# Decay sums of both triangles side by side in two-part products, key blocks on ScalarE, two gate weights off GpSimd, constants loaded in the first stage

## The chip, the cores and the metric

The kernel runs on one core of a Trainium2 chip. The metric is device time in microseconds (us), the median of several executions of the whole kernel. A profiled execution gives the trace: each instruction's start and duration on TensorE (PE), VectorE (DVE), ScalarE (ACT), GpSimd (POOL) and SyncE (SP), which here only issues transfers.

## The reference

One layer of a decoder works on 512 prompt tokens and 8 x 4 sample tokens with one set of weights. Half of its heads are sparse attention (NSA), half gated linear attention (GLA); then come an output projection, a gated feed-forward part, and a per-layer embedding gate. What matters here is the GLA part, whose decays are sums of logarithms within chunks of 32 tokens, and the mixer's output:

```python
def step(S, blk):
    qc, kc, vc, ac = blk
    b = jnp.cumsum(ac, axis=1)
    qe = qc * jnp.exp(b)
    ke = kc * jnp.exp(-b)
    att = jnp.where(causal, jnp.einsum('bihd,bjhd->bhij', qe, ke), 0.0)
    o = jnp.einsum('bhij,bjhv->bihv', att, vc) + jnp.einsum('bihd,bhdv->bihv', qe, S)
    b_last = b[:, -1]
    kd = kc * jnp.exp(b_last[:, None] - b)
    S = S * jnp.exp(b_last)[..., None] + jnp.einsum('bjhd,bjhv->bhdv', kd, vc)
    return S, o
...
o_g = (rmsnorm(o_gla, gla_norm) * jax.nn.silu(g_gla)).reshape(B, T, GLA_V_DIM)
return jnp.concatenate([o_nsa, o_g], axis=-1) @ w_o
```

The last step of all is `rmsnorm(h, norm_final)`, whose result is the output yT.

## The kernel before

Activations stand with features on the partitions: 1024 features are 8 tiles of 128, and the 544 columns (512 prompt, 32 sample) are worked in two halves of 256 and 288. Projections are exact to float32 by two parts: a weight tile `wraw` of 128 x 1024 is split into `wh` and `wl`, activations into `xh` and `xl`, and three products (wh xh, wh xl, wl xh) of a reduced-precision float32 type are added in PSUM (`acc3`). The split of a weight is a cast on ScalarE and a subtraction on VectorE, or, with `lo=POOL`, both on GpSimd, the subtraction in four pieces (`load_w`). A product of plain float32 shows two records in the trace.

The work is staged: input statistics, NSA projections and key compression; scores and softmax of the prompt; GLA projections (`pj` tiles of qg, kg, vg); the GLA stage; the output projection (`pk`); the feed-forward part (`pg`, `pu`, `pd`); embedding gate and final norm. Each engine has one queue and works it in order. A scheduler sets the order of each queue from the program and from priorities; `tc.issue_after` and `together` tie some instructions to others.

In the GLA stage stand side by side:

- The four gate weights gg0 to gg3 (`tile_gg`): each is fetched one ahead (`raws`), split on GpSimd, and multiplied with all 544 columns; `ev_silu` makes the gate `om_g` of it.
- The sample values (`s_values`): score tiles are transposed (`sT`, `pT`) and multiplied with value pages `vch` into `sO`. For each row of four pages SyncE loads three and GpSimd gathers one (`load_page`, `gather_page`); there are four buffers. The result is copied to `Os` on ScalarE and transposed (`sOT`).
- The GLA itself. The log decays `ls` come back from DRAM. `sps` are the sums for the sample tokens, with the small triangle `tri4`. For each pair of heads (ip 0 and 1) `gla_front` makes the sums for the prompt with two triangles, `bps` and `rps`, their exponentials `E`, `En`, `X`, and the transposed keys (`kdp`, then X again); `gla_states` copies the keys of each of four blocks into a block-diagonal tile `kdz` (L1095: four copies of 32 rows, two on GpSimd, two on ScalarE), multiplies them with the values (`U`, PSUM) and chains the states S on VectorE; `gla_out` makes the outputs (`go`, `U`), their norms (`og`, `gst`: square, sum, power, scaling; the power is on GpSimd) and `gla_gate` transposes them (`ogp`) and multiplies them with the gate. The sample tokens' part (`oiq`, `oip`, `vb`, `kd`) uses `bmask`, `glah` and `tri4`.

After it, the mixer's output is split again into `xh2` and `xl2`, which take over the buffers of `xh` and `xl`, and the first products of `pk` run on the parts of the first 256 columns that are there (`early_k`). In the last stage `finish` scales h by the broadcast reciprocal norm `bc` and stores it.

Of the kernel before, what the change touches and what calls it, by code (L numbers as in the profile page):

```python
# [9 lines left out]
F32 = mybir.dt.float32  # L10
F32R = mybir.dt.float32r
I32 = mybir.dt.int32
AF = mybir.ActivationFunctionType
ALU = mybir.AluOpType
# [21 lines left out]
def kernel(ctx: ExitStack, tc: tile.TileContext, i: dict, o: dict):  # L36
# [591 lines left out]
    later[3][1]()  # L628
    compress_prompt()
# [372 lines left out]
    def tile_gg(j, lo=POOL):  # L1002
        w = load_w(None, 1024, lo, raw=raws[j])
        if j < 3:
            raws.append(fetch(i["win_fm"][FM.index(f"gg{j + 1}")], 1024))
        fm_tile(None, ev_silu(j), w, then=tick)
# [6 lines left out]
    tri4 = gp.tile([32, 3, 32], F32, name="tri4")  # L1013
    SP.dma_start(tri4, i["tri4"])
    bmask = gp.tile([128, 8], F32, name="bmask")
    SP.dma_start(bmask, i["bmask"])
    glan = gp.tile([128, 1], F32, name="glan")
    SP.dma_start(glan, i["glan"])
    glah = gp.tile([128, 1], F32, name="glah")
    DVE.tensor_scalar_mul(glah, glan, 0.5)  # L1020
# [39 lines left out]

    def gla_front(ip):
        cs = slice(ip * 128, ip * 128 + 128)
        bps, rps = g1("bps"), g1("rps")
        for t in range(4):
            mm(bps[:, t * 128:t * 128 + 128], ls[:, t, cs], tri[:, 0, :])
# [3 lines left out]
        ACT.activation(E, bps, AF.Exp, scale=-1.0)  # L1069
        ACT.activation(En, bps, AF.Exp)  # L1070
        for t in range(4):
            mm(rps[:, t * 128:t * 128 + 128], ls[:, t, cs], tri[:, 1, :])
        ACT.activation(X, rps, AF.Exp, scale=-1.0)
# [14 lines left out]
    def gla_states(ip, ec, kdt):  # L1088
        S = gp.tile([128, 17, 128], F32, name="S", bufs=2)
        POOL.memset(S[:, 0, :], 0.0)  # L1090
        for t in range(4):
            kz = kdz[t % 2]
            for c in range(4):
                cp_ = slice(32 * c, 32 * c + 32)
                (ACT.copy if c % 2 else POOL.tensor_copy)(kz[cp_, c, :], kdt[cp_, t, :])  # L1095
# [127 lines left out]

    def split_o(k, hf):
# [9 lines left out]
    def early_k(k0, k1):  # L1234
        for mt in range(2):
            for k in range(k0, k1):
                acc3(parts[mt], HALF[0][1], w_wo[mt], k, xh2, xl2, k, 0, k == 0, False)
# [3 lines left out]
    for k in range(4):  # L1241
        split_o(k, 0)
    w_wo = [load_w(i["wo"][mt], 1024) for mt in range(2)]
# [3 lines left out]
    early_k(0, 4)  # L1247
    for k in (4, 5):
        split_o(k, 0)
# [171 lines left out]
    def finish(dg, hf):  # L1421
# [4 lines left out]
        ACT.copy(r[:, :n], bc[:, :n])  # L1426
        ys = [pl_.tile([128, 2, 288], F32, name="y", bufs=5) for _ in range(5)]
        where = {0: (0, 0), 4: (2, 0), 1: (1, 0), 5: (2, 1), 2: (3, 0), 3: (3, 1), 6: (4, 0), 7: (4, 1)}
        for k, (z, j) in where.items():
# [183 lines left out]
```

## Time and profile before

| | |
|---|---|
| runs | 907.25, 898.73, 907.13 us (median 907.13) |
| profiled execution | 902.78 us, its span 901.0 us |
| TensorE busy | 857.9 us, 95% of the span |
| VectorE, ScalarE, GpSimd busy | 55%, 40%, 17% |
| mean granted clock of TensorE | 0.98 of full speed |

The span runs from the first to the last instruction of the core; the executions' time has 1.8 us around it. A busy share is a mean over all stages. The granted clock is given as a share of 2.4 GHz; 0.5 is the lower level of 1.2 GHz. In a row of the timeline the number in brackets is the engine's idle time ahead of it, with what ended it.

### The profile page before, as it was taken

How to read it: one execution, taken by the hardware profiler on the slowest of the kernel's cores; microseconds unless marked ns; L12 is line 12 of the kernel's file. 1: busy time of each engine (PE TensorE's matmuls, PEld its weight loads, DVE VectorE, ACT ScalarE, POOL GpSimd, SP SyncE). 2: the span in 40 equal slices, each digit the busy share in tenths (PEclk: the TensorE clock that was granted, in tenths of full speed). 3: DMA queues.
4: the chain of work that ended last, by engine and by line, in shares of the span. 5: the costliest groups of instructions: out<-in, count | busy, mean ns of one | idle time of the engine just before them, and what ended most of it. 6: DMA issues, size and time to landing. Idle time of an engine off the chain costs nothing.

```text
span 901.0 us, 18098 instructions
## 1 busy us (share of the span) xinstructions
PE 857.9 (95%) x6872; PEld 794.4 (88%) x6872; DVE 496.4 (55%) x1204; ACT 364.7 (40%) x898; POOL 151.6 (17%) x196
## 2 busy tenths in 40 slices
PE   5999999999999988899999999999999999999995
PEld 5899987777777756799999999999999999999994
DVE  6646367778665634584555555555554333335654
ACT  7344377678755501452332323333232222224322
POOL 3544153000026215250000000000000000002511
PEclk9999999999998969999999999999999999999998
DMA  8677423232205232561233333322223232234111
GB/s 253 190 228 214 126 79 113 80 101 60 92 2 169 84 122 71 169 235 60 83 111 101 117 118 117 109 96 101 75 90 85 88 105 77 86 103 142 48 54 47
DMA packets 58822, 99.09 MB, mean 110 GB/s; under 512 B 11319, under 2 KB 40264, under 8 KB 58352
## 3 DMA queue, kind: packets, MB, share of 16 engines
q1 hardware_dynamic: 55296, 90.33, 31.5%
q0 software_dynamic: 2192, 5.90, 2.3%
q10 hardware_dynamic: 1248, 1.70, 0.5%
q8 instruction: 54, 0.88, 0.4%
q14 instruction: 32, 0.26, 0.1%
HBM read 91.74 MB, written 10.37 MB: 113 GB/s over the span
## 4 chain that ended last, share of the span: by engine, by line
PE 79%; DVE 6%; issue 4%; POOL 4%; ACT 3%; DMA 2%; SPq 1%; DVEq 0%; POOLq 0%; ACTq 0%
PE pg L57 17%; PE pd L57 15%; PE pu L57 15%; PE pj L57 9%; PE pk L57 5%; PE cps L57 4%; PE sc L57 3%; PE pO L57 2%; PE pT L776 2%; PE U L57 2%; PE go L57 1%; POOL xc L98 1%; DVE xl L259 1%; PE sS L57 1%; PE sO L57 1%
## 5 line engine op out<-in xcount | busy, mean ns | idle before, releaser
L132 ACT CAST wh<-wraw 128x1024 fp32r<-128x1024 f32 (+1 forms) x89 | 91.6, 1030 | 166.9 <-issue 73.9
L137 DVE TENSOR_TENSOR wl<-wraw,wh 128x1024 fp32r<-128x1024 f32 (+1 forms) x85 | 101.8, 1198 | 87.7 <-ACT wh L132 86.8
L57 PE MATMUL pg<-xh,wh 128*128 128x256 f32 (+1 forms) x400 | 115.7, 289 | 0.0
L57 PE MATMUL pg<-xl,wh 128*128 128x256 f32 (+1 forms) x400 | 115.2, 288 | 0.0
L57 PE MATMUL pg<-xh,wl 128*128 128x256 f32 (+1 forms) x400 | 114.6, 286 | 0.0
L57 PE MATMUL pd<-hh,wl 128*128 128x256 f32 (+1 forms) x352 | 101.8, 289 | 0.0
L57 PE MATMUL pd<-hl,wh 128*128 128x256 f32 (+1 forms) x352 | 101.6, 289 | 0.0
L57 PE MATMUL pd<-hh,wh 128*128 128x256 f32 (+1 forms) x352 | 101.6, 289 | 0.0
L57 PE MATMUL pu<-xh,wh 128*128 128x256 f32 (+1 forms) x352 | 101.5, 288 | 0.0
L57 PE MATMUL pu<-xl,wh 128*128 128x256 f32 (+1 forms) x352 | 101.3, 288 | 0.0
L57 PE MATMUL pu<-xh,wl 128*128 128x256 f32 (+1 forms) x352 | 100.8, 286 | 0.0
L57 PE MATMUL pj<-xh,wh 128*128 128x256 f32 (+1 forms) x272 | 82.0, 304 | 10.0 <-ACT wh L132 8.1
L176 POOL TENSOR_TENSOR prs<-pst,mhalf 128x2 f32<-128x2 f32 (+1 forms) x9 | 6.0, 672 | 451.8 <-DVE pst L175 451.8
L57 PE MATMUL pj<-xl,wh 128*128 128x256 f32 (+1 forms) x272 | 80.5, 298 | 0.0
L57 PE MATMUL pj<-xh,wl 128*128 128x256 f32 (+1 forms) x256 | 76.9, 300 | 1.3 <-DVE wl L137 1.2
L57 PEld LDWEIGHTS pg<-xh,wl 128*128 128x128 f32 x400 | 75.3, 188 | 0.0
L57 PEld LDWEIGHTS pg<-xl,wh 128*128 128x128 f32 x400 | 75.1, 188 | 0.0
L57 PEld LDWEIGHTS pg<-xh,wh 128*128 128x128 f32 x400 | 75.0, 188 | 0.1
L57 PEld LDWEIGHTS pd<-hh,wh 128*128 128x128 f32 x352 | 66.3, 188 | 0.1
L57 PEld LDWEIGHTS pu<-xh,wl 128*128 128x128 f32 x352 | 66.3, 188 | 0.0
L57 PEld LDWEIGHTS pd<-hl,wh 128*128 128x128 f32 x352 | 66.3, 188 | 0.0
L57 PEld LDWEIGHTS pd<-hh,wl 128*128 128x128 f32 x352 | 66.2, 188 | 0.0
(400 smaller groups left out, 2065.9 us busy)
## 6 DMA issues: line engine op xcount, KB each, us to landing
wraw<-in_wg SPq DMA_DIRECT2D x22, 512.0 KB, 3.4
wraw<-in_wu SPq DMA_DIRECT2D x22, 512.0 KB, 3.3
wraw<-in_win_fm SPq DMA_DIRECT2D x17, 512.0 KB, 3.3
wraw<-in_wd SPq DMA_DIRECT2D x16, 512.0 KB, 3.5
xc<-in_pgc SPq DMA_DIRECT2D x32, 128.0 KB, 2.6
kch<-in_pgk SPq DMA_DIRECT2D x64, 64.0 KB, 2.0
wraw<-in_wo SPq DMA_DIRECT2D x8, 512.0 KB, 4.2
wraw<-in_wpg SPq DMA_DIRECT2D x8, 512.0 KB, 4.1
```

The costliest lines, as they stand in the source:

```text
L57: pe[0] = PE.matmul(out, lhsT, rhs, start=start, stop=stop)
L98: return POOL.indirect_dma_start(out=dst, out_offset=None, in_=src.rearrange("a p c -> (a p) c"), in_offset=bass.IndirectOffsetOnAxis(ap=p ...
L132: ACT.copy(wh[:, :n], raw[:, :n])
L137: lo_[0] = DVE.tensor_sub(wl[:, :n], raw[:, :n], wh[:, :n])
L176: POOL.tensor_tensor(r[0:m, b:e], a[0:m, b:e], mhalf[0:m, b:e], op=ALU.pow)
L259: DVE.scalar_tensor_tensor(xl[:, k, c0:c1], v, gk, xh[:, k, c0:c1], op0=ALU.mult, op1=ALU.subtract)
L776: PE.transpose(tp[:, 128 * r:128 * r + 128], Ps[r][b][:, 128 * kt:128 * kt + 128], ident)
```

## The change

1. `tri4`, `bmask` and `glan` are loaded in the first stage and not in the GLA stage; `glah` is made there too.
2. `ls` is split into two parts (`lsh` by a cast on ScalarE, `lsl` on VectorE in place), the two triangles are cast side by side into `trr`, and each block of 128 columns takes two products of 128 x 256 (`brs`) for both triangles. The six exponentials of a pair are of 128 x 256 (three of 128 x 512 before), X first.
3. All copies into `kdz` are on ScalarE.
4. gg2 and gg3 are split on ScalarE and VectorE; gg3's call fetches the first tile of wo.
5. The two parts of the first four tiles of the mixer's output, first half, go to buffers of `E` and `En` (`split_first`), from which the first products of `pk` read; GpSimd copies them to xh2 and xl2 later, for the other products.
6. In `finish` for the last half, VectorE scales six tiles from the PSUM tile `bc` itself; a second broadcast serves the copy for GpSimd's two (three before). Stores go to SyncE's and ScalarE's queues in turn.

```diff
@@ -626,6 +626,14 @@
     later[2][1]()
     fm_tile("q1", ev_q(1), then=lambda hf: block(5 + hf))
     later[3][1]()
+    tri4 = op_.tile([32, 3, 32], F32, name="tri4")
+    SP.dma_start(tri4, i["tri4"])
+    bmask = op_.tile([128, 8], F32, name="bmask")
+    SP.dma_start(bmask, i["bmask"])
+    glan = op_.tile([128, 1], F32, name="glan")
+    SP.dma_start(glan, i["glan"])
+    glah = op_.tile([128, 1], F32, name="glah")
+    DVE.tensor_scalar_mul(glah, glan, 0.5)
     compress_prompt()
     gates()
     wg3 = decay_factors()
@@ -999,10 +1007,9 @@
     raws = [fetch(i["win_fm"][FM.index("gg0")], 1024)]
-    def tile_gg(j, lo=POOL):
-        w = load_w(None, 1024, lo, raw=raws[j])
-        if j < 3:
-            raws.append(fetch(i["win_fm"][FM.index(f"gg{j + 1}")], 1024))
+    def tile_gg(j):
+        w = load_w(None, 1024, POOL if j < 2 else None, raw=raws[j])
+        raws.append(fetch(i["win_fm"][FM.index(f"gg{j + 1}")] if j < 3 else i["wo"][0], 1024))
         fm_tile(None, ev_silu(j), w, then=tick)
@@ -1010,14 +1017,6 @@
     SP.dma_start(ls, lsd)
     tri = gp.tile([128, 3, 128], F32, name="tri")
     SP.dma_start(tri, i["tri"])
-    tri4 = gp.tile([32, 3, 32], F32, name="tri4")
-    SP.dma_start(tri4, i["tri4"])
-    bmask = gp.tile([128, 8], F32, name="bmask")
-    SP.dma_start(bmask, i["bmask"])
-    glan = gp.tile([128, 1], F32, name="glan")
-    SP.dma_start(glan, i["glan"])
-    glah = gp.tile([128, 1], F32, name="glah")
-    DVE.tensor_scalar_mul(glah, glan, 0.5)
     qs = gp.tile([128, 2, NS], F32, name="qs")
@@ -1058,19 +1057,34 @@
     for z in range(2):
         POOL.memset(kdz[z], 0.0)
+    lst = gp.tile([128, 1280], F32R, name="lst", tag="S", bufs=2)
+    lsh, trr = lst[:, 0:1024].rearrange("p (t c) -> p t c", t=4), lst[:, 1024:1280]
+    lsl = ls[:, 0:4, :].bitcast(F32R)
+    ACT.copy(trr, tri[:, 0:2, :].rearrange("p a c -> p (a c)"))
+    ACT.copy(lsh, ls[:, 0:4, :])
+    DVE.tensor_sub(lsl, ls[:, 0:4, :], lsh)
     def gla_front(ip):
         cs = slice(ip * 128, ip * 128 + 128)
-        bps, rps = g1("bps"), g1("rps")
-        for t in range(4):
-            mm(bps[:, t * 128:t * 128 + 128], ls[:, t, cs], tri[:, 0, :])
+        both = []
+        for z in range(2):
+            ps = g1("brs")
+            for t in range(2):
+                for w in (lsh, lsl):
+                    mm(ps[:, 256 * t:256 * t + 256], w[:, 2 * z + t, cs], trr, start=w is lsh, stop=w is lsl)
+            both.append(ps.rearrange("p (t a c) -> p a t c", t=2, a=2))
+        def half(t, z):
+            return t[:, 256 * z:256 * z + 256].rearrange("p (t c) -> p t c", t=2)
         E = gp.tile([128, SEQ], F32, name="E", bufs=2)
         En = gp.tile([128, SEQ], F32, name="En", bufs=2)
         X = gp.tile([128, SEQ], F32, name="X", bufs=1)
-        ACT.activation(E, bps, AF.Exp, scale=-1.0)
-        ACT.activation(En, bps, AF.Exp)
-        for t in range(4):
-            mm(rps[:, t * 128:t * 128 + 128], ls[:, t, cs], tri[:, 1, :])
-        ACT.activation(X, rps, AF.Exp, scale=-1.0)
+        for z in range(2):
+            ACT.activation(half(X, z), both[z][:, 1], AF.Exp, scale=-1.0)
+            ACT.activation(half(E, z), both[z][:, 0], AF.Exp, scale=-1.0)
+            ACT.activation(half(En, z), both[z][:, 0], AF.Exp)
         DVE.tensor_mul(X, kg[:, ip, :SEQ], X)
         kdp = g1("kdp")
         for t in range(4):
@@ -1092,7 +1106,7 @@
             kz = kdz[t % 2]
             for c in range(4):
                 cp_ = slice(32 * c, 32 * c + 32)
-                (ACT.copy if c % 2 else POOL.tensor_copy)(kz[cp_, c, :], kdt[cp_, t, :])
+                ACT.copy(kz[cp_, c, :], kdt[cp_, t, :])
             U = psu.tile([128, 512], F32, name="U", tag="U", bufs=2)
             for c in range(4):
                 for hh in range(2):
@@ -1221,6 +1235,15 @@
     for hd in (2, 3):
         tile_gg(hd)
+    def split_first():
+        t = [[gp.tile([128, 512], F32R, name="o" + tag, tag=tag, bufs=2) for _ in range(2)] for tag in ("E", "En")]
+        ehi, elo = ([u[:, 256 * z:256 * z + 256] for u in part for z in range(2)] for part in t)
+        for k in range(4):
+            ACT.copy(ehi[k], om_n[:, k, 0:256])
+            DVE.tensor_sub(elo[k], om_n[:, k, 0:256], ehi[k])
+        return ehi, elo
     def split_o(k, hf):
         c0, c1 = HALF[hf]
         src = om_n[:, k, c0:c1] if k < 4 else om_g[:, k - 4, c0:c1]
@@ -1234,17 +1257,25 @@
     def early_k(k0, k1):
         for mt in range(2):
             for k in range(k0, k1):
-                acc3(parts[mt], HALF[0][1], w_wo[mt], k, xh2, xl2, k, 0, k == 0, False)
+                if k < 4:
+                    wh, wl = (t[:, 128 * k:128 * k + 128] for t in w_wo[mt])
+                    mm(parts[mt][:, 0:256], wh, ehi[k], start=k == 0, stop=False)
+                    mm(parts[mt][:, 0:256], wh, elo[k], start=False, stop=False)
+                    mm(parts[mt][:, 0:256], wl, ehi[k], start=False, stop=False)
+                else:
+                    acc3(parts[mt], HALF[0][1], w_wo[mt], k, xh2, xl2, k, 0, False, False)
     xh2 = xp.tile([128, KT, TT], F32R, name="xh2", tag="xh")
     xl2 = xp.tile([128, KT, TT], F32R, name="xl2", tag="xl")
-    for k in range(4):
-        split_o(k, 0)
-    w_wo = [load_w(i["wo"][mt], 1024) for mt in range(2)]
+    ehi, elo = split_first()
+    w_wo = [load_w(None, 1024, raw=raws[4]), load_w(i["wo"][1], 1024)]
     for hd in (2, 3):
         gla_gate(hd, ogs[hd])
     parts = [early_o(mt) for mt in range(2)]
     early_k(0, 4)
+    for k in range(4):
+        POOL.tensor_copy(xh2[:, k, 0:256], ehi[k])
+        POOL.tensor_copy(xl2[:, k, 0:256], elo[k])
     for k in (4, 5):
         split_o(k, 0)
     early_k(4, 6)
@@ -1423,9 +1454,21 @@
         n = c1 - c0
         bc = bcast(nm, dg, hf)
         r = fp.tile([128, 288], F32, name="nrs", bufs=2)
-        ACT.copy(r[:, :n], bc[:, :n])
+        ACT.copy(r[:, :n], (bc if hf else bcast(nm, dg, hf))[:, :n])
         ys = [pl_.tile([128, 2, 288], F32, name="y", bufs=5) for _ in range(5)]
         where = {0: (0, 0), 4: (2, 0), 1: (1, 0), 5: (2, 1), 2: (3, 0), 3: (3, 1), 6: (4, 0), 7: (4, 1)}
+        if not hf:
+            for z, (ks, eng) in enumerate((((0,), SP), ((5, 4), ACT), ((1, 2), SP), ((7, 6), ACT), ((3,), SP))):
+                k0 = min(ks)
+                for k in ks:
+                    y, src, gk = ys[z][:, k - k0, :n], h[:, k, c0:c1], gcols[:, 3, k:k + 1]
+                    if k in (5, 7):
+                        POOL.tensor_tensor(y, src, r[:, :n], op=ALU.mult)
+                    else:
+                        DVE.scalar_tensor_tensor(y, src, 1.0 if k in POST else gk, bc[:, :n], op0=ALU.mult, op1=ALU.mult)
+                eng.dma_start(o["yT"][:, k0:k0 + len(ks), c0:c1], ys[z][:, :len(ks), :n])
+            return
         for k, (z, j) in where.items():
             y, src, gk = ys[z][:, j, :n], h[:, k, c0:c1], gcols[:, 3, k:k + 1]
             if k in POST:
```

GpSimd, between the second pair's key blocks and the end of the GLA outputs; `vch` are gathers of value pages, `gst` the powers of the output's norm, `wh` and `wl` the parts of gg3. Before:

```order
L98 DMA vch<-in_pgv,pidx 128x128
L1095 COPY kdz_4266<-X 32x128
L98 DMA vch<-in_pgv,pidx 128x128
L1095 COPY kdz_4267<-X 32x128
L98 DMA vch<-in_pgv,pidx 128x128
L1095 COPY kdz_4267<-X 32x128
L98 DMA vch<-in_pgv,pidx 128x128
L1138 TENSOR_TENSOR gst<-gst,mhalf 128x4 x2
L98 DMA vch<-in_pgv,pidx 128x128 x3
L130 TENSOR_SCALAR wh<-wraw 128x1024
L135 TENSOR_TENSOR wl<-wraw,wh 128x256 x4
L1138 TENSOR_TENSOR gst<-gst,mhalf 128x4
```

After, from the memsets of the states on to the first copy of the output's parts (`oE`, `oEn` are the new buffers):

```order
L1104 MEMSET S 128x128
L98 DMA vch<-in_pgv,pidx 128x128 x4
L1214 TENSOR_TENSOR sst<-sst,mhalf 128x1
L1104 MEMSET S 128x128
L98 DMA vch<-in_pgv,pidx 128x128 x7
L1152 TENSOR_TENSOR gst<-gst,mhalf 128x4 x2
L98 DMA vch<-in_pgv,pidx 128x128
L1152 TENSOR_TENSOR gst<-gst,mhalf 128x4 x2
L1278 COPY xl_5731<-oEn 128x256
```

Key blocks and the split of gg3 are gone from the row, gathers and powers stand alone, and the copies for xh2 and xl2 come behind them.

TensorE, from the second pair's last decay sums to the transposition of X (`kdp`); `pj` are products of gate tiles. Before:

```order
L57 MATMUL rps<-tri,ls 128x128 x3
L57 MATMUL pj<-xh,wl 128x288
L57 MATMUL pj<-xh,wh 128x288
L57 MATMUL pj<-xl,wh 128x288
L57 MATMUL pj<-xh,wl 128x288
L57 MATMUL sO<-vch,pT 32x128 x4
L57 MATMUL pj<-xh,wh 128x288
L57 MATMUL pj<-xl,wh 128x288
L57 MATMUL pj<-xh,wl 128x288
L961 MATMUL sT<-c_ident,Ps 72x128
L1077 MATMUL kdp<-c_ident,X 128x128 x4
```

After:

```order
L57 MATMUL brs<-lst 128x256
L57 MATMUL brs<-lst,ls 128x256
L57 MATMUL brs<-lst 128x256
L57 MATMUL brs<-lst,ls 128x256
L57 MATMUL U<-vg,kdz_4266 64x128 x4
L57 MATMUL sO<-vch,pT 32x128 x4
L57 MATMUL U<-vg,kdz_4266 64x128 x4
L1091 MATMUL kdp<-c_ident,X 128x128 x3
L57 MATMUL U<-vg,kdz_4267 64x128 x7
```

The gate products have moved away from this place; block products U and value products sO stand between sums and transposition.

TensorE, from the sample's sums `sps` to the scores `attps` of the sample tokens. Before:

```order
L57 MATMUL sps<-tri_4216,ls 128x32 x4
L57 MATMUL pj<-xh,wh 128x288
L57 MATMUL pj<-xl,wh 128x288
L57 MATMUL pj<-xh,wl 128x288
L57 MATMUL pj<-xh,wh 128x288
L57 MATMUL attps<-qs,ksm 32x32
L57 MATMUL pj<-xl,wh 128x288
L57 MATMUL pj<-xh,wl 128x288
L961 MATMUL sT<-c_ident,Ps 128x128
L57 MATMUL attps<-qs,ksm 32x32
```

After, the beginning of the same piece, in which fourteen `pj` follow on `sps`:

```order
L57 MATMUL sps<-tri_1443,ls 128x32 x4
L57 MATMUL pj<-xl,wh 128x288
L57 MATMUL pj<-xh,wl 128x288
L57 MATMUL pj<-xh,wh 128x288
L57 MATMUL pj<-xl,wh 128x288
L57 MATMUL pj<-xh,wl 128x288
```

The sums stand nine gate products further ahead, and more of these follow before anything that depends on the sums.

## Rows read from the trace of the kernel before

**Rows 1.** Windows from 262 to 373 us: busy time and operations by engine, clock, DMA.

```profile
262.00:280.00 18.00, 16.02 (x118) 13.01 (x116) 10.03 (x28) 6.77 (x22) 13.46 (x20) 0.95 0.51 172
...
300.00:320.00 20.00, 18.41 (x215) 12.94 (x214) 12.40 (x36) 7.05 (x20) 4.60 (x12) 0.98 0.28 86
320.00:340.00 20.00, 16.82 (x143) 11.10 (x142) 6.33 (x16) 1.08 (x2) 5.09 (x7) 0.60 0.36 119
340.00:360.00 20.00, 16.97 (x191) 13.60 (x188) 8.61 (x18) 2.53 (x5) 9.89 (x11) 0.92 0.27 80
360.00:373.00 13.00, 10.32 (x107) 7.54 (x107) 6.41 (x15) 5.77 (x15) 0.00 (x0) 1.00 0.35 121
```

**Rows 2.** Windows cut at the changes of the granted clock, same columns.

```profile
278.10:285.00 6.90, 6.52 (x35) 5.39 (x35) 4.35 (x9) 4.21 (x13) 5.67 (x8) 0.51 0.45 126
319.10:336.20 17.10, 14.40 (x119) 9.18 (x116) 3.67 (x10) 0.91 (x2) 3.47 (x5) 0.50 0.44 144
356.60:360.10 3.50, 3.15 (x19) 3.14 (x16) 1.27 (x3) 0.44 (x1) 0.00 (x0) 0.51 0.52 173
```

**Rows 3.** TensorE's waits from 262 to 385 us: total, times, longest.

```profile
PE U L57 <- POOL kdz L1095: 4.1, 3, 2.1
PE sT L961 <- DVE om_g L944: 2.0, 1, 2.0
PE sps L57 <- DMA tri<-in_tri: 1.3, 1, 1.3
PE sOT L988 <- ACT Os L986: 1.1, 1, 1.1
```

**Rows 4.** GpSimd's timeline: start, duration, what, and the idle before it in brackets.

```profile
323.84 0.28 POOL L1095 COPY kdz<-X 32x128 f32<-32x128 f32 x1 [1.84 <-DMA vch<-in_pgv,pidx]
...
348.36 2.80 POOL L135 TENSOR_TENSOR wl<-wraw,wh 128x256 fp32r<-128x256 f32 x4
```

**Rows 5.** Groups on ScalarE by form, 262 to 384 us: busy, mean ns, idle before.

```profile
L1095 ACT COPY kdz<-X 32x128 f32<-32x128 f32 x16 | 4.7, 295 | 2.7 <-PE U L57 2.2
...
L132 ACT CAST wh<-wraw 128x1024 fp32r<-128x1024 f32 x3 | 3.1, 1049 | 0.0
...
L1069 ACT ACTIVATE E<-bps 128x512 f32<-128x512 f32 x2 | 1.2, 600 | 3.2 <-PE bps L57 3.2
```

**Rows 6.** Timelines of VectorE and TensorE, one row each.

```profile
371.50 1.22 DVE L137 TENSOR_TENSOR wl<-wraw,wh 128x1024 fp32r<-128x1024 f32 x1
...
312.32 0.66 PE L57 MATMUL U<-vg,kdz 128*64 128x128 f32 x8
```

**Rows 7.** The chain that ended last, decay sums: start, duration, what.

```profile
281.08 1.71 PE bps L57 x8
282.79 1.71 PE rps L57 x8
...
303.22 0.86 PE bps L57 x6
```

**Rows 8.** The chain, 415 to 440 us: products of a gate tile.

```profile
421.89 2.85 PE pg L57 x24
```

**Rows 9.** The chain, 262 to 385 us: a load's landing.

```profile
270.64 4.69 DMA tri<-in_tri
```

**Rows 10.** SyncE's timeline, first stage and GLA stage.

```profile
54.41 0.36 SPq L633 DMA_DIRECT2D rowv<-in_rowv  x1
...
57.74 1.94 SPq L104 DMA_DIRECT2D xc<-in_pgc  x4
...
269.68 0.44 SPq L1010 DMA_DIRECT2D ls<-lsd  x1
...
273.45 27.81 SPq L104 DMA_DIRECT2D vch<-in_pgv  x24
```

**Rows 11.** The last stage on all engines, in order of time.

```profile
888.38 0.42 DVE L1451 SCALAR_TENSOR_TENSOR ft<-ft,pp 128x256 f32<-128x256 f32 x1 [0.48 <-ACT ft L1450]
...
893.22 0.37 ACT L1426 COPY nrs<-bc 128x256 f32<-128x256 f32 x1 [2.97 <-PE bc L57]
...
893.62 3.56 DVE L1434 SCALAR_TENSOR_TENSOR y<-h,gcols,nrs 128x256 f32<-128x256 f32 x5 [1.54 <-ACT nrs L1426]
```

## The prediction

> **What bounds the kernel now.** I read the busy time by stretches first, then the granted clock, then who is waited for, then the waiting rows themselves. TensorE is the bound: after the mixer it runs without a gap at full clock to the last stage. What a change can win lies where it idles or is slowed, and that is the stretch from 262 to 373 us, in which the gated linear attention (GLA), the last gate weights and the sample values run. The five windows that hold all its idle time [rows 1] show 1.98, 1.59, 3.18, 3.03 and 2.68 us of it, together 12.5 us. The clock column shows a second loss: in three pieces TensorE was granted 1.2 instead of 2.4 GHz [rows 2]. Half of its busy time in them is lost: 6.52 x 0.49, 14.40 x 0.50 and 3.15 x 0.49, so 3.2 + 7.2 + 1.5 = 11.9 us. Each piece begins close behind a wait of TensorE. So 24 us of a stretch of 111 could be had if nothing were waited for. Who is waited for [rows 3]: GpSimd's copies of key blocks 4.1 us in three waits, the gated output 2.0 us, the small constants 1.3 us, ScalarE's copy Os 1.1 us. Behind the first stand the gathers of value pages on GpSimd: ahead of the copy at 323.84 it idles 1.84 us until a gather lands, as it takes its work in order [rows 4]. Behind the second stands the split of a gate weight on GpSimd, whose four subtractions alone take 2.80 us [rows 4], ahead of the small power operations that the GLA output needs.
>
> **The change part by part.**
> *Key blocks on ScalarE.* 16 copies of 0.295 us join 16 of the same kind there [rows 5], so a block of four costs ScalarE 1.18 us where two engines shared it. The 4.1 us of waits on GpSimd go, since ScalarE waits for no gather. What is late next is ScalarE itself: TensorE's eight products of a block, sixteen records, take 2 x 0.66 us [rows 6], about the same, and other products stand between the blocks. I leave 0.7 us of such waits (0, if these always cover; 8 x 0.59 = 4.7 us, if two of the four copies stay uncovered in each of the eight blocks).
> *Gate weights.* The third and fourth now cost ScalarE a cast of 1.05 us [rows 5] and VectorE a subtraction of 1.22 us each [rows 6], where GpSimd took 2.80 and more. ScalarE is busy 7.05 of 20 us in 300 to 320 and 1.08 in 320 to 340 [rows 1], so they fit; but the third's cast stands just ahead of the first block's exponentials, which may wait for it, up to 1 us. The 2.0 us wait on the gated output goes; I keep 0.5 us of it, for the square, sum, power and scaling that still run between product and transposition.
> *Decay sums.* Sixteen records of 128 columns per head pair become eight of 256. Before: 1.71 us for each triangle of the first pair at half clock, and in the second 0.86 for six at full clock [rows 7], so 2.3 for sixteen; 5.7 together. After: a 128 x 256 product costs 2.85 / 24 = 0.119 us at full clock [rows 8], so 0.95 a pair, 1.9 if the clock is halved; 2.85 with the first at half. That is 2.9 us on TensorE's own path. Against it: the parts must be made first. A cast of 1.05 us and a subtraction of 1.22 [rows 5, 6] stand between the landing of ls and the first product; TensorE has some 24 projection products there now, more than 2.3 us at 0.119. The cast also stands ahead of the exponentials of the sample's sums: 0.3 us (0 to 1). Then the six half-size exponentials: X is complete after the fourth, each between half of 0.60 and 0.60 us [rows 5]. In the second pair the order puts only eight block products and four short ones between the sums and the transposition of X; before, projection products stood there. I add 0.7 us of waiting in the first pair and 1.4 in the second, 2.1 (0 to 4).
> *Constants.* Before, the small triangle, issued third, landed at 270.64 + 4.69 = 275.33 us [rows 9]; ls was issued first, 1 us ahead [rows 10], and lands sooner by that at most; I take 0.6. The sums of the sample move nine products ahead, so TensorE comes about 9 x 0.134 = 1.2 us earlier and waits longer, 1.3 + 1.2 - 0.6 = 1.9 us, with the nine products still to be done then. So the stage goes on 0.6 us sooner, in line with an idle sum that has the 1.9 in it; I claim no more. In the first stage three issues join SyncE's row of small loads; these end at 54.77 and the next page loads begin at 57.74 [rows 10], so three issues of 0.44 us, 1.3, are covered by 3.0 us without an issue. If the page loads turn out to be late, that is what it costs.
> *First output parts into E and En.* TensorE waits 1.1 us for Os, because casts that themselves wait for the last projection stand ahead of it on ScalarE. The new buffers don't wait for that projection. I keep 0.5 of the 1.1. What comes in: eight GpSimd copies between the last power operation and the split of the next weight, nowhere in this trace; the nearest rows are the four subtractions of one size, 2.80 / 4 = 0.70 [rows 4], so 5.6 us, or less if a copy reads only one operand. TensorE has two output tiles of work ahead, 48 products of 256 and 48 of 288 columns, about 12 us at 0.119 and up. Covered; I charge 0.4 us (0 to 3).
> *The tail.* The scaled rows begin when the broadcast is out, not after the copy of 0.37 us. Five rows on VectorE took 3.56 us, 0.71 each, beside GpSimd's; the same size alone, with one operand in PSUM, took 0.42 [rows 11]. Six rows now: 6 x 0.42 = 2.5, or 6 x 0.71 = 4.3. Start 0.4 earlier, so the end moves by +1.5 to -0.3 us; a smaller last transfer and a second queue add up to half a microsecond. I take 1.2 us, near the upper bound, since the operand in PSUM is what the 0.42 row has. The Trainium skill, "SBUF — State Buffer", on the two separate sides, says that a VectorE operation with two SBUF inputs and a GpSimd operation that reads SBUF share a port pair, of which one holds it for its whole instruction. By that rule the six rows, now with one SBUF input, are free of GpSimd: the gain would be 1.5; without it, nothing.
>
> **The sum.** Idle that stays: 1.9 (sample sums) + 2.1 (X) + 0.7 (key blocks) + 0.5 (gated output) + 0.5 (Os), and half of the 4.0 us that the four named waits leave of the 12.5, which are short waits for ScalarE's and VectorE's readings: 7.7 us, so 4.8 won. Clock: the pieces at 319 and 356 follow waits that go, 7.2 + 1.5; the one at 278 follows a wait that stays, and I leave another short piece of 1.7 us, the size of the third, since new waits come in. So 7.0 won. Then 2.9 for the sums, 1.2 for the tail, less 0.4 and 0.3. Together 4.8 + 7.0 + 2.9 + 1.2 - 0.7 = 15.2 us. The profiled execution took 902.78 us (a span of 901.0 and 1.8 around it): 887.6, so **888 us**. The other runs were 898.73, 907.13 and 907.25, with a median 4.4 above the profiled one, so against that median the same sum gives 892; the range has to hold both.
>
> **Rivals.**
> *The clock is halved again elsewhere.* TensorE's wait at the sample sums becomes longer, and short products of 32 and 128 columns follow it. If a half-clock piece of the length of 319 to 336 comes up in the new order, 7.0 less 1.7 are not won: 893 to 896. For it: the longest waits of that stretch each had one behind them [rows 2, 3]. Against it: the wait of 1.1 us for Os had none. The Trainium skill, "TensorE: Matmul & The Clock Gate", Part 1, describes such a gate, driven by activity. The traces agree that the clock falls after idle time, and cannot say how little would do.
> *ScalarE takes GpSimd's place.* Key blocks, exponentials and casts in one order on one engine: waits of 4.7 us at the blocks and 4 at X, the upper bounds above, take 5.9 more than forecast, and the long half-clock piece comes back with them, 5.5 to 7: 899 to 901. Against it: ScalarE's 7.05 of 20 us.
> *Value pages set the pace.* SyncE issues 24 loads in 27.81 us [rows 10], 48 in all. From 271.4 on, with the window loads, they cannot end before about 335, and their data not before 338. My sum puts the last value products near 354, 14 us ahead of 368. If the buffers' releases delay them, 3 to 5 us are lost: 891 to 893.
> *Slower than before.* One mechanism: the half clock holds from the sample sums through the GLA output. Its price is the busy time at half: to lose the 15 us that are won takes 30 us more of it than forecast, so some 40 us in all between 275 and 345; to be 1% slower, about 58. The longest here is 17.1 us [rows 2]. Then 907 to 918.
>
> **How the numbers follow.** Forecast 0.48; the clock rival 0.20; ScalarE 0.12; pages 0.08; no second half-clock piece, or not even the first, 878 to 885, 0.06; slower 0.06. The range takes in the bounds of X, blocks and tail below (879) and all but the end of the ScalarE case above: 878 to 900. A change under 1%, about 9 us, is what a measurement of this kernel can't tell from none; below 898 lie the forecast, both mild rivals and a part of ScalarE's, so faster 0.77, same 0.17, slower 0.06.
>
> **What would show it.** Waits on GpSimd's key blocks gone, and no wait of over 1 us for ScalarE's; full clock from 319 on; sums of 0.95 us a pair; dense output products from about 358 instead of 372.8; y rows of 0.42 us. I am wrong if the clock column shows a long half-clock piece, if X or kdz from ScalarE leads the waits, or if the dense part after 373 itself has become longer.

## The result, and the profile after

The changed kernel takes **889.39 us** (median of four runs, 887.43 to 891.20), the kernel before 905.65 in the same comparison: a ratio of 0.9837, interval 0.9802 to 0.9871, so 1.6 % less. The profiled execution took 891.20 us, a span of 889.4.

The windows of the profile after, with the same columns as [rows 1, 2]: six stretches of the GLA stage; then the two pieces at half clock up to the end of that stage, and what follows the second of them.

```profile
262.00:280.00 18.00, 15.98 (x123) 13.21 (x122) 8.82 (x29) 9.77 (x32) 9.51 (x13) 0.99 0.33 100
280.00:300.00 20.00, 19.60 (x194) 15.98 (x194) 13.21 (x33) 14.78 (x54) 7.90 (x10) 0.92 0.42 126
300.00:320.00 20.00, 19.45 (x241) 13.47 (x239) 14.74 (x43) 14.39 (x50) 5.11 (x7) 1.00 0.36 98
320.00:340.00 20.00, 19.17 (x239) 13.04 (x240) 10.83 (x26) 4.53 (x9) 4.36 (x5) 1.00 0.44 141
340.00:360.00 20.00, 17.30 (x171) 13.06 (x169) 9.87 (x23) 4.66 (x11) 6.25 (x10) 1.00 0.43 128
360.00:373.00 13.00, 12.29 (x101) 12.27 (x101) 11.37 (x22) 6.46 (x15) 8.76 (x10) 1.00 0.66 217
...
132.80:139.70 6.90, 6.90 (x28) 6.51 (x29) 1.54 (x12) 3.77 (x14) 0.00 (x0) 0.51 0.59 188
279.60:283.10 3.50, 3.50 (x16) 3.44 (x16) 3.27 (x5) 2.04 (x10) 3.21 (x5) 0.51 1.04 336
283.10:407.00 123.90, 118.70 (x1197) 98.69 (x1195) 80.51 (x182) 58.10 (x156) 40.52 (x49) 1.00 0.46 142
```

The first six lines hold 2.02, 0.40, 0.55, 0.83, 2.70 and 0.71 us of idle TensorE, 7.2 together where 12.5 was. From 283 us on the clock is full (last line); of the three half-clock pieces of [rows 2] one short one is left. ScalarE shows what the change asked of it: 14.39 of 20 us at 300 to 320, twice its earlier 7.05. The line at 132.80 is new, 6.9 us at 1.2 GHz in the stage before, whose code the change doesn't touch.

TensorE's waits after, 262 to 385 us (total, times, longest), against [rows 3]:

```profile
PE sps L57 <- DMA ls<-lsd: 1.7, 1, 1.7
PE pk L57 <- ACT wh L132: 1.5, 1, 1.5
PE pj L57 <- DVE om_g L952: 1.0, 3, 0.4
PE pk L57 <- DVE wl L137: 0.7, 1, 0.7
PE pj L57 <- ACT pT L971: 0.7, 1, 0.7
PE kdp L1091 <- DVE X L1088: 0.6, 1, 0.6
PE sOT L996 <- DVE atts L1130: 0.5, 1, 0.5
PE go L57 <- DVE og L1157: 0.4, 1, 0.4
```

No wait on a key block is left, on either engine, and Os is gone. In their place come the sample's sums (1.7 us, now waiting for `ls` itself), the cast of a weight ahead of the output products (1.5) and X (0.6).

I measure the GLA stage in every trace from TensorE's first transposition of the sample's scores (`sT`) to the first broadcast `bc` of the feed-forward norm: 270.63 to 418.12 us before, 274.61 to 406.68 after, so 147.5 and 132.1. That is 15.4 us won. The stage begins 4.0 us later in the changed kernel: TensorE is 0.6 us behind from its first product on, loses 3.1 more in the piece at 132.8 and 0.3 behind it. Nothing is lost where the three small loads are now issued, near 55 us. The stretch from `bc` to the last stage's `bc` is alike within 0.3, and the tail lost 0.1: 11.6 us between the two profiled executions.

### The profile page after: what moved, and what is told of

The parts are those of the page before. It is cut to its first block, busy times and chain, and to the rows that moved or that the text cites. A ratio compares the mean times of both kernels' runs of the same rounds, so it can differ in the third digit from the quotient of the medians.

```text
span 889.4 us, 18081 instructions
## 1 busy us (share of the span) xinstructions
PE 852.3 (96%) x6858; PEld 790.7 (89%) x6858; DVE 498.2 (56%) x1208; ACT 372.3 (42%) x924; POOL 142.1 (16%) x177
## 4 chain that ended last, share of the span: by engine, by line
PE 79%; DVE 6%; issue 5%; ACT 4%; DMA 3%; POOL 3%; SPq 1%; POOLq 0%; DVEq 0%; ACTq 0%
PE pg L57 17%; PE pu L57 15%; PE pd L57 15%; PE pj L57 9%; PE pk L57 5%; PE cps L57 4%; PE sc L57 2%; PE pO L57 2%; PE U L57 2%; PE pT L784 2%; PE sO L57 1%; POOL xc L98 1%; PE go L57 1%; DVE wl L137 1%; PE sS L57 1%
## 5 line engine op out<-in xcount | busy, mean ns | idle before, releaser
L132 ACT CAST wh<-wraw 128x1024 fp32r<-128x1024 f32 (+1 forms) x91 | 93.8, 1030 | 167.9 <-issue 74.3
L137 DVE TENSOR_TENSOR wl<-wraw,wh 128x1024 fp32r<-128x1024 f32 (+1 forms) x87 | 104.5, 1201 | 88.0 <-ACT wh L132 87.1
L57 PEld LDWEIGHTS pj<-xh,wh 128*128 128x128 f32 x272 | 53.8, 198 | 14.5 <-ACT wh L132 8.7
```

The costliest lines, as they stand in the source:

```text
L57: pe[0] = PE.matmul(out, lhsT, rhs, start=start, stop=stop)
L132: ACT.copy(wh[:, :n], raw[:, :n])
L137: lo_[0] = DVE.tensor_sub(wl[:, :n], raw[:, :n], wh[:, :n])
```

## The experiments

Twelve kernels ran, on three chips, on which the kernel before took 907.18, 907.48 and 907.94 us. So times are compared by their ratio to the kernel before on the same chip, and traces by the stage as defined above. Columns: ratio and interval; median granted clock of the timed runs; then of the one trace: length of the stage, idle of TensorE in it, time at half clock in it, all in us.

| kernel | ratio | clock | stage | idle | at half clock |
|---|---|---|---|---|---|
| before | 1 | 0.981 | 147.5 | 12.4 | 27.3 |
| changed | 0.9837 (0.9802 to 0.9871) | 0.992 | 132.1 | 7.2 | 3.4 |
| e9_changed_again | 0.9891 (0.9839 to 0.9943) | 0.991 | 133.2 | 7.6 | 3.4 |
| e1_blocks_back | 0.9897 (0.9861 to 0.9933) | 0.989 | 134.6 | 6.2 | 6.8 |
| e2_gates_back | 0.9922 (0.9886 to 0.9958) | 0.989 | 132.5 | 8.2 | 0 |
| e3_both_back | 0.9900 (0.9862 to 0.9938) | 0.985 | 136.4 | 6.2 | 10.2 |
| e4_gpsimd_alone | 0.9905 (0.9872 to 0.9939) | 0.986 | 136.1 | 7.5 | 6.8 |
| e5_sums_alone | 0.9957 (0.9921 to 0.9992) | 0.980 | 139.6 | 7.1 | 20.5 |
| e6_sums_back | 0.9977 (0.9948 to 1.0006) | 0.981 | 140.9 | 7.5 | 23.9 |
| e7_split_back | 0.9929 (0.9895 to 0.9963) | 0.985 | 133.4 | 7.7 | 3.4 |
| e8_constants_back | 0.9915 (0.9890 to 0.9941) | 0.987 | 136.3 | 7.6 | 10.2 |
| e10_gate_first | 0.9952 (0.9927 to 0.9977) | 0.985 | 139.5 | 8.4 | 13.7 |
| e11_gate_first_tail | 0.9935 (0.9909 to 0.9960) | 0.986 | 140.1 | 8.8 | 13.7 |
| e12_filled_wait | 0.9947 (0.9921 to 0.9973) | 0.986 | 139.5 | 9.0 | 10.2 |

**The control, e9_changed_again,** is the changed kernel once more, unedited.

> The changed kernel as it is, on the chip of the next three. All theories: GLA stage 132 us within 1, with no half-clock piece between 300 us and the feed-forward part; ratio to the kernel before 0.980 to 0.988.

All three expectations were missed, the stage and the ratio by a little. Its stage came out 1.1 us longer than the first trace's, with some 0.5 us more idle; its half-clock piece lies at 365.75 instead of 279.60, and another one at 92.69. Its runs at a clock of 0.992 took 893.50 to 894.26 us, the one at 0.980 took 904.07. So a difference of stages below some 1.5 us means nothing, and neither does a single short piece.

The part ahead of the stage varies more: it took 270.6 to 281.9 us in the fourteen traces, and 270.6, 279.0, 278.7 and 273.8 in the kernel before and in e4, e5 and e12, which differ from it only behind that part. Stage and time can therefore disagree: e5's stage is 7.9 us shorter than before, its time 0.43 %, 3.9 us. A stage rests on one trace, a ratio on four to twelve runs; where they disagree, the ratio counts.

**What does relieving GpSimd do? e1, e2, e3 take it back, e4 does it alone.** The edit of e1 (e3 has both this and the next):

```diff
-                ACT.copy(kz[cp_, c, :], kdt[cp_, t, :])
+                (ACT.copy if c % 2 else POOL.tensor_copy)(kz[cp_, c, :], kdt[cp_, t, :])
```

> The changed kernel with half of the key-block copies on GpSimd again, all else kept. Theory (TensorE lost time behind GpSimd's queue, and again behind the half clock that follows such waits): the gathers of value pages still stand in that queue, so waits of 2 to 4 us on GpSimd's kdz come back between 300 and 330 us, and at least one half-clock piece in that stretch; 893 to 899 us against 889 for the changed kernel. Rival (the split of the gate weights was what kept GpSimd late, so its queue is short enough now): waits on kdz under 0.5 us in sum, full clock from 300 us on, 888 to 890.

The edit of e2, in `tile_gg`:

```diff
-        w = load_w(None, 1024, POOL if j < 2 else None, raw=raws[j])
+        w = load_w(None, 1024, POOL, raw=raws[j])
```

> The changed kernel with the third and fourth gate weight split on GpSimd again, all else kept. Theory: the fourth weight's split, 3.85 us, stands ahead of the powers of the output's norm again, so a wait of about 2 us on the gated output comes back around 345 us, perhaps with a half-clock piece of 3.4 us (1.7 lost); 891 to 894 us. Rival (key blocks off GpSimd give its queue room enough): no wait of over 1 us on the gated output, 888 to 890.

> The changed kernel with both, half of the key-block copies and the two gate weights, on GpSimd again; the two-part decay sums, the early constants, the first output parts and the tail are kept. Theory: of the 16 us won, GpSimd's waits (4.1 + 2.0 before) and the half clock behind them (8.7) are the larger part, so 897 to 903 us, with one or two half-clock pieces after 300 us. Rival (the win is in the decay sums and the order that they bring): 889 to 893.

The kernel e4 is the kernel before with the two lines as the change has them, and nothing else:

> The kernel before with only these two edits: all key-block copies on ScalarE, third and fourth gate weight on ScalarE and VectorE. Theory: the larger part of the win comes with them, 892 to 898 us against about 905, full clock from 300 us on and no wait on GpSimd's kdz. Rival (ScalarE takes GpSimd's place or the win is in the sums): 902 to 906, with waits on ScalarE's kdz or X of over 2 us in sum.

TensorE's wait on key blocks in e1:

```profile
PE U L57 <- POOL kdz L1109: 1.0, 1, 1.0
```

The waits on GpSimd's blocks did not return in their old size with its copies: there is one of 1.0 us in e1 and one of 0.9 in e3, against 4.1 in three before, and no half-clock piece between 300 and 330 us. So the theory of e1 was wrong, and so was that of e2, in which no wait on `om_g` is over 0.8 us. The 900.40 us of e3 lie in the 897 to 903 of its theory, but the waits that it named did not come, and by the control's ratio the changed kernel itself would take an estimated 897.3 on that chip (0.9891 x 907.18). Taking both back costs the stage 3.2 us against the control, with 6.8 us more at half clock, and the ratio of e3 can't be told from the control's. Yet e4 alone takes 11.4 us off the stage before and 0.95 % off the time, with no wait on key blocks and full clock from 300 us on, as its theory said. So the relief is worth much in the old order, and in the new one no more than these runs can tell from nothing. My reason for it, that gathers on GpSimd hold up the copies that TensorE waits for, held only in the order of before. Why the other parts cover the same waits is argued and not shown: in the new order other products stand between the second pair's blocks.

**What do the sums do? e5 does them alone in the kernel before** (the block that makes `lst`, and the new front part of `gla_front`), **e6 takes them back in the changed kernel.**

```diff
# e5, on the kernel before; e6 is the reverse, on the changed kernel
+    lst = gp.tile([128, 1280], F32R, name="lst", tag="S", bufs=2)
...
-        bps, rps = g1("bps"), g1("rps")
...
+        for z in range(2):
+            ps = g1("brs")
...
```

> The kernel before with the two-part decay sums alone; GpSimd keeps key blocks and gate weights. Measured on the GLA stage (TensorE's first transposition of sample scores to its first broadcast of the feed-forward norm: 147.5 us before, 132.1 changed). New theory after the first four runs (either the relief of GpSimd or a new order, in which output products stand among the second pair's block products, hides the waits for key blocks): in this kernel's order the first output product stands 16 rows ahead of the last block product, so the waits on kdz fall under 1.5 us and the long half-clock piece goes: 136 to 140 us, 895 to 899 in all. Old theory (the sums are worth their own products, 2 to 3 us): 144 to 146, 902 to 904, with 3 us or more of waits on kdz.

> The changed kernel with the four-product float32 decay sums of before, all else kept. Both theories: the products cost 2.7 us more at full clock, up to 4.2 with the first pair at half clock, and the waits for X change by less than 1 us: GLA stage 134 to 137 us, 891 to 894 in all. If the sums matter through the order alone (GpSimd is relieved here, so nothing is to be hidden), 132 to 133.

Here the ratios separate: e6 lies at 0.9948 to 1.0006, the control at 0.9839 to 0.9943. Without the sums nearly nothing of the change is left, though by themselves they were put at 2.9 us. Both expectations for e6 missed it, 134 to 137 and 132 to 133 us for a stage of 140.9. Of e5's new theory the waits on key blocks and the stage came as said (none, and 139.6 us), but a long half-clock piece is there, at another place. In the traces, TensorE's busy time in the stage is 8.5 us more in e6 than in the changed kernel; some 2.5 of that are the products, the rest the clock. The traces show where. Timeline of TensorE in e6, then the windows of its half-clock pieces (columns as above); PE rows give start, duration, what, and the idle before in brackets:

```profile
338.70 0.46 PE L57 MATMUL go<-vg,atts 128*128 128x128 f32 x2 [1.08 <-DVE og L1142]
...
340.54 0.39 PE L57 MATMUL U<-vg,atts 128*128 128x128 f32 x2
340.86 0.65 PE L57 MATMUL U<-S,E 64*32 64x128 f32 x8
341.44 0.79 PE L57 MATMUL U<-vg,atts 128*128 128x128 f32 x2
...
351.62 0.66 PE L57 MATMUL sO<-VT,pT 72*32 72x128 f32 x8 [3.26 <-DVE pT L973]
```

```profile
286.20:293.10 6.90, 6.90 (x34) 5.99 (x34) 3.86 (x11) 2.12 (x12) 4.70 (x6) 0.51 0.85 253
340.80:357.90 17.10, 13.50 (x116) 9.30 (x115) 7.35 (x17) 3.34 (x7) 4.98 (x5) 0.50 0.21 64
```

And the same place in e5:

```profile
334.93 0.46 PE L57 MATMUL go<-vg,atts 128*128 128x128 f32 x2 [2.16 <-DVE og L1158]
335.31 0.42 PE L57 MATMUL go<-S,E 64*32 64x128 f32 x8
335.67 0.49 PE L57 MATMUL go<-vg,atts 128*128 128x128 f32 x2
```

```profile
336.90:347.00 10.10, 10.10 (x83) 6.90 (x83) 3.19 (x10) 1.66 (x4) 1.83 (x2) 0.50 0.08 21
```

In both, TensorE waits for the first pair's scaled output `og` (1.08 and 2.16 us), goes on with narrow products and is halved two microseconds later, for 17.1 and 10.1 us. In the changed kernel, e6 and e5 alike TensorE goes on with `go` 2.9 to 3.0 us after the scores `att` of the second pair; what differs is what lies over this time. In the changed kernel it is thirteen gate products with a wait of 0.47 among them and one of 0.36 at the end, and no long piece follows. In e6 it is thirteen and then 1.08 in one, in e5 four and 2.16. Before, the long piece at 319 also came behind a wait ahead of narrow products, there 1.4 us for a key block, which ended at 318.77. The two pieces of 17.1 us hold a further wait, 2.1 us for a key block before and 3.3 us for `pT` in e6, the largest of that stage; its copy stands behind the scaling of the second outputs on VectorE. The piece of 10.1 us holds none. Not every such wait has a piece behind it: those of 1.0 and 0.9 us ahead of block products in e1 and e3, and one of 0.8 ahead of output products in e8, have none. That the piece comes from the wait is what e12 tries.

**e12_filled_wait:** the kernel e5 with ten useless products of 96 x 512 ahead of the second pair's `go`; added work that nothing reads.

```diff
+        if ip:
+            with tc.issue_after(pe[0].ins):
+                fill = g1("fill")
+                for _ in range(10):
+                    mm(fill, kd3[:, 0, :], vs3)
         for attp in attps:
```

> The kernel before with the two-part sums alone, and ten products of 96 x 128 x 512, 2.2 us of added work whose result nothing reads, just where TensorE waited 2.2 us for the second output's norm. Theory (that wait makes the half-clock piece of 10.2 us behind it, 5 us lost): the piece goes, and the GLA stage takes 134 to 136.5 us instead of 139.6, although work is added. Rival (the narrow output products themselves let the clock fall, or the wait has nothing to do with it): 139 to 142, with the piece still there.

TensorE's timeline, and its waits in the stage:

```profile
328.82 2.57 PE L57 MATMUL fill<-vs,kd 96*128 96x512 f32 x10 [0.79 <-DVE atts L1136]
331.23 0.39 PE L57 MATMUL go<-vg,atts 128*128 128x128 f32 x2
```

```profile
PE pk L57 <- ACT wh L132: 2.0, 2, 1.6
PE sO L57 <- DMA vch<-in_pgv: 1.7, 3, 1.1
PE pj L57 <- DVE om_g L944: 1.6, 4, 0.7
```

The wait for `og` and the piece of 10.1 us are both gone, and the median clock of the timed runs is 0.986 against e5's 0.980, each beside 0.981 of the kernel before on its chip. So in this kernel filling the wait keeps the clock up; the order of the narrow products behind it also changed a little. But the stage is 139.5 us as in e5: TensorE's busy time in it fell by 2.0 us, the added work included, and its idle time rose by 1.9. 3.1 us were won by the first transposition of the outputs (`ogp` 63.0 us after `sT`, 66.1 in e5), and lost again to the waits of the second fence, on a weight's cast, value pages and the gates' first step `om_g`, at most 0.8 in sum for each in e5. My 134 to 136.5 was wrong, and the rival's piece did not come: faster products there only ran into what comes later.

**The two smaller parts. e7** puts `for k in range(4): split_o(k, 0)` in the place of `split_first` and leaves the GpSimd copies out; **e8** moves the three small loads and `glah` back behind `tri`.

```diff
# e7
-    ehi, elo = split_first()
+    for k in range(4):
+        split_o(k, 0)
...
# e8, behind the load of tri
+    tri4 = gp.tile([32, 3, 32], F32, name="tri4")
+    SP.dma_start(tri4, i["tri4"])
...
```

> The changed kernel without the buffers for the first output parts: these wait for the last gate products again. Theory: ScalarE's casts stand ahead of Os and of the weight's cast again, 0.5 to 1.5 us more of waits around the first output products, GLA stage 132.5 to 134 us. Rival (the first output tile's weight is late anyway, as the 1.5 us wait for its cast in the changed kernel says): 131.5 to 132.5.

> The changed kernel with the three small loads in the GLA stage again. The sample's sums then stand nine gate products later in TensorE's order. Theory (the part is worth the 0.6 us of the landing at most): GLA stage 132 to 133 us, the wait at the sums shorter than 1.7 us by about 0.6. Rival (the first stage pays for the three loads): the GLA stage as said, but the time up to it shorter by 1 us.

Both ratios overlap the control's, so neither part is shown to matter by itself. In e7's trace the wait for the weight cast grows from 1.5 to 2.1 us, no more; the wait for Os doesn't come back, so the new buffers were not what removed it. In e8 the sums wait 1.2 us for the small triangle `tri4` instead of 1.6 for `ls` in the control, and TensorE meets a wait of 2.6 us for window values that the changed kernel doesn't have; the stage is 3.1 us longer than the control's, more than I had allowed, and what the three loads have to do with that stays open.

**Can the largest wait left be had? e10** moves the first gate tile in behind the load of `ls`, so that its products lie over the 1.7 us at `sps`. **e11** is e10 with the whole last scaling on VectorE.

```diff
# e10 and e11
     SP.dma_start(ls, lsd)
+    tile_gg(0)
...
-    for hd in (0, 1):
-        tile_gg(hd)
+    tile_gg(1)
...
# e11 alone, in finish
-                    if k in (5, 7):
-                        POOL.tensor_tensor(y, src, r[:, :n], op=ALU.mult)
-                    else:
-                        DVE.scalar_tensor_tensor(y, src, 1.0 if k in POST else gk, bc[:, :n], op0=ALU.mult, op1=ALU.mult)
+                    DVE.scalar_tensor_tensor(y, src, 1.0 if k in POST else gk, bc[:, :n], op0=ALU.mult, op1=ALU.mult)
```

> The changed kernel with the first gate tile called ahead of the sample's decay sums, so that all its 24 products of the second half stand ahead of these sums in TensorE's order. Theory (a wait of TensorE costs itself and the half clock behind it, unless wide products are left to fill it): the wait of 1.7 us for ls goes, and the half-clock piece of 3.4 us behind it (1.7 us lost): GLA stage 129 to 131 us, 1.5 to 3 us faster than the changed kernel. Rival (these products are missed later): a wait of over 1 us at the second pair's output products with a long half-clock piece behind it, 134 to 140.

> As the kernel with the first gate tile ahead, and in the last half all eight output rows on VectorE from the broadcast, without the second broadcast, the copy and GpSimd's rows. Theory (GpSimd's closing drain, which ends 4.1 us after its last row, ends the changed kernel; the last transfer is done 0.7 us sooner): from the last broadcast to the end 8.2 us instead of 8.9. Rival (the transfers set the end, and two more rows on VectorE delay the last of them by 0.8): 8.9 or more.

The first waits of TensorE in e10:

```profile
PE sO L57 <- DMA vch<-in_pgv: 3.4, 2, 2.2
PE pj L57 <- DVE om_g L952: 2.2, 2, 2.0
```

The wait at `sps` is gone, and the gate products it took are missing further on: 5.6 us of waits on value pages and on `om_g`, the gates' first step, 13.7 us at half clock in three pieces, a stage 6.3 us longer than the control's. The ratio, 0.9952, points the same way; its interval still overlaps the control's by 0.0016. So the rival of that run held in its sum, though not in its place: no wait of over 1 us stands at the second pair's output products, and no piece is longer than 6.9 us. The wait of 1.7 us is cheap where it stands.

The tail, from the last stage's last `bc` to the end of the span, is 8.5 us in e10 (891.96 to 900.5) and 7.3 in e11 (892.14 to 899.4). The last stage after, in order of time on all engines, then e11's:

```profile
880.53 2.04 PE L57 MATMUL bc<-ndg,ones 128*128 128x256 f32 x4 [1.64 <-DVE ndg L178]
881.77 0.48 DVE L1469 SCALAR_TENSOR_TENSOR y<-h,gcols,bc 128x256 f32<-128x256 f32 x1 [1.38 <-PE bc L57]
882.16 0.41 DVE L1469 SCALAR_TENSOR_TENSOR y<-h,bc 128x256 f32<-128x256 f32 x1
882.27 2.24 SPq L1470 DMA_DIRECT2D out_yT<-y  x3
882.50 1.65 DVE L1469 SCALAR_TENSOR_TENSOR y<-h,gcols,bc 128x256 f32<-128x256 f32 x4
882.67 0.37 ACT L1457 COPY nrs<-bc 128x256 f32<-128x256 f32 x1 [4.12 <-PE bc L57]
883.12 1.41 POOL L1467 TENSOR_TENSOR y<-h,nrs 128x256 f32<-128x256 f32 x2 [3.25 <-ACT nrs L1457]
```

```profile
892.14 0.67 PE L57 MATMUL bc<-ndg,ones 128*128 128x256 f32 x2 [1.64 <-DVE ndg L178]
...
893.35 2.90 SPq L1468 DMA_DIRECT2D out_yT<-y  x3
...
895.02 0.86 DVE L1467 SCALAR_TENSOR_TENSOR y<-h,gcols,bc 128x256 f32<-128x256 f32 x2
```

After, VectorE is done at 884.15, but GpSimd's two rows wait for the copy of the second broadcast and end at 884.53, and its closing drain ends at 888.63, 4.1 us behind its last row; SyncE's queue had finished at 887.97. With no row left on GpSimd (e11), its drain ends at 895.58, SyncE at 898.6, and the tail is 1.2 us shorter than in e10, where 0.7 was expected, though VectorE now has eight rows. The other thirteen tails are 8.0 to 9.1 us.

## Why the prediction held, and where a term did not

**The total: near, with luck in it.** The sum took 15.2 us off the profiled 902.78. Between the two profiled executions 11.6 came: the GLA stage gave 15.4 where the sum had 14.0 for it, the tail lost 0.1 where it had 1.2, and 4.0 went ahead of the stage, where it had nothing. That the median of 889.39 lies so near to 888 is chance in part: the same kernel took 895.92 on another chip, which the range also holds.

**Idle time: the right sum from other waits.** 4.8 us were put down, 5.3 came (12.5 to 7.2). The named terms: sample sums 1.9, measured 1.7; key blocks 0.7, none; gated output 0.5, none at that place; Os 0.5, none listed; X 2.1, measured 0.6 in one wait. They came to 2.3 us instead of 5.7, and the waits left unnamed to 4.9 instead of 2.0, among them 1.5 for the cast of a weight on ScalarE ahead of the output products. The dense output products begin near 362 us, 358 with the later start of the stage taken off, as forecast. The three loads of the constants were covered, as said.

**Decay sums: right in size.** The eight products of the second pair start 0.118 us apart. TensorE's timeline and, for the first pair, the chain:

```profile
306.37 0.39 PE L57 MATMUL brs<-lst 128*128 128x256 f32 x1
...
307.30 0.28 PE L57 MATMUL brs<-lst,ls 128*128 128x256 f32 x1
```

```profile
287.37 0.48 PE brs L57 x4
...
288.19 0.67 PE brs L57 x4
```

That is 0.95 and 1.15 us, at full clock in both pairs, for 2.3 before at that clock. What I did not see is that the clock makes more of them than their length does (e6).

**Clock: the right sum from a wrong price.** TensorE's busy time in the stage fell by 10.1 us (135.05 to 124.91); 2.5 of it are the sums at full clock, so about 7.6 the clock, for 7.0 forecast. Yet 23.9 us of half clock went, which at my price of one half would have given 10.2. That step, "half of its busy time in them is lost", is too dear: products don't take twice as long there. Gate products of 288 columns, after, at half and at full clock:

```profile
280.54 0.44 PE L57 MATMUL pj<-xh,wh 128*128 128x288 f32 x1
280.78 0.44 PE L57 MATMUL pj<-xl,wh 128*128 128x288 f32 x1
...
300.00 0.29 PE L57 MATMUL pj<-xh,wh 128*128 128x288 f32 x1
300.13 0.29 PE L57 MATMUL pj<-xl,wh 128*128 128x288 f32 x1
```

They start 0.24 us apart instead of 0.13, so 45 % is lost. Narrow ones lose about 40 %: behind eight `go<-S,E` the next product starts after 0.36 us at full clock (e5, above), behind eight `U<-S,E` after 0.58 in e6's halved piece. With these shares an estimate from [rows 2] gives about 8.5 us; why 7.6 came stays open. And I expected two pieces to stay, 3.2 and 1.7 us lost; one short one did, which the control shows to be luck. The rivals of the clock and of slower had their mechanism in e5 and e6: a wait ahead of narrow products, and ten to seventeen microseconds at half clock behind it.

**ScalarE as the new bound: no.** Sixteen more copies at 0.295 us, as expected; the group on ScalarE, with the idle before it:

```profile
L1109 ACT COPY kdz<-X 32x128 f32<-32x128 f32 x32 | 9.4, 295 | 1.0 <-PE U L57 0.2
```

TensorE has no wait on these copies; what it waits for on ScalarE is the weight's cast. **Value pages: not here,** but e10, e11 and e12 show 1.7 to 4.4 us of waits on them, and e8 2.6 on the window values, as soon as the order shifts: they stand close behind.

**The tail: the failed term.** The rows came as forecast: 0.48, 0.41 and 1.65 for four, 2.54 us for six, so 0.42 each beside GpSimd's rows with the operand in PSUM, where five took 0.71 each [rows 11]. This agrees with the rule of the Trainium skill, "SBUF — State Buffer", on the two separate sides. But "I take 1.2 us" counted VectorE's rows as the end, and between these two traces nothing was gained: 8.8 us before (892.23 to 901.0), 8.9 after. Before, GpSimd's closing drain (900.21) and SyncE's queue (900.23) ended together, so sooner stores alone could win nothing. After, SyncE's queue ends 7.4 us behind `bc` instead of 8.0, but GpSimd's rows start later (2.59 us after `bc`, 1.4 before), since a second broadcast and a copy stand ahead of them, and its drain ends the run. The clock at `bc` has a part in it: the four products take 2.04 us after, at half clock, and 1.10 in e2, at full clock, whose tail is 8.0. At like clock the new tail is 0.2 to 0.6 us shorter: halved all along, 8.9 against 9.1 in e12, which has the old tail; at full, 8.0 against 8.6 in e4, which has it too.

**Whose gain it is** does not read as a sum of parts. In the single traces the relief alone takes 11.4 us of the stage, all but the relief 11.1, the sums alone 7.9, all but the sums 6.6. The ratios are less clear: 0.95, 1.00, 0.43 and 0.23 % off the time, each within about 0.4, against 1.6 and 1.1 for the whole. They show that without the sums little is left, and no more. Idle falls to 6.2 to 7.5 us in all four, so each removes most of the waits on key blocks; they differ in what stays at half clock. Not run: the changed kernel with e11's tail, which by an estimate from e10 and e11 should take about 1 us more off. Open is what decides a single short piece, why e8's stage grew, and how the sums shorten the wait for `og` in the changed kernel but not in e5.

## What to carry to other kernels

Where one engine runs against several late helpers, cost the waits together: here, in single traces, edits that by themselves took 8 and 11 us off the stage took 14 to 15 off together with the rest. Ask of every wait what wide work the order still has to lay over it: three stalls of 1.1 to 2.2 us ahead of narrow products were followed by a much longer time at half clock, though shorter ones were not, and moving the filler forward, or adding some, only opened later gaps. Compare medians of many runs and not single traces, since code that no edit touched moved by some 8 us between them. At the very end of a kernel give the engine that closes slowest no work at all.

## What the runs showed of the hardware that I had not expected

The clock is halved also where nothing changed: at 132.80 for 6.9 us after, at 92.69 in the control, at neither place before; and one file's runs spread from 893.50 to 904.07 us with a clock of 0.992 to 0.980. Of the time at half clock some 40 to 45 % is lost here, not half. GpSimd's closing drain ends 4.1 us after its last row, before and after alike.
